# A hybrid encoder layer on one core: heads' products in pairs, weights loaded by events, a third fill tile, packed constants, five prepared down steps

## The chip, the cores and the metric

One core of one Trainium2 chip. The metric is the device time of one execution in microseconds. TensorE (PE) multiplies, VectorE (DVE) and ScalarE (ACT) work on tiles in SBUF and PSUM, GpSimd (POOL) does small steps, and SyncE (SP) issues nearly all transfers, in its own order.

## What is computed

One encoder layer over 16 tiles of 128 positions (two sequences of 1024, model width 1024). The core of the reference:

```python
h = rms_norm(x, norm1)
q, k, v, gu, gv = split(h @ w_in)                 # widths 512, 128, 128, 512, 512
a = rms_norm(windowed_gqa(q, k, v, q_gain, k_gain, sink, rel_table), attn_out_gain)
g = rms_norm(chunked_spatial_gating(gu, gv, v_gain, w_s, b_s), gmlp_out_gain)
x = x + concatenate([a, g]) @ w_o
h2 = rms_norm(x, norm2)
x = x + (silu(h2 @ w_gate) * (h2 @ w_up)) @ w_down   # inner width 2816
...
# windowed_gqa: 8 heads of 64, 2 key/value heads, block of 128 queries against 3 blocks of keys
scores = q . k / sqrt(64) + bias[rel], masked to |rel| <= 128
e = exp(scores - m);  probs = e / (sum(e) + exp(sink - m));  out = probs @ v
```

## The kernel before

Every product is made of three: operands are split into a high and a low part by `split` or `split_gain` (L111 on ScalarE gives the high part, L112 on VectorE the low one), and `mm3` (L221 to L223) multiplies high by high, low by high and high by low. In the projections these are fp32 forms, in the products of probabilities with v (L484 to L486) and in the FFN f16 forms.

**Start.** For k = 0 to 7 the k-th slice of x of the first four tiles and of the q weights (`load_wq`) is loaded, split and multiplied. Seven small constants come in by seven transfers: g1s on SP, the others on POOL's queue. Then the bias of relative positions is built: a row of it is written to DRAM, read back shifted, and turned by eight products (`bias_turn`, L291, L292).

**Attention.** A list of events, each with a time, is sorted and then run; the order of the calls is the order on every engine. `AT` holds the offsets, and tile t's work is put at 8 t plus an offset. Per tile: load and split x (`load_x`, L180, `split_x_hi`, L185), project it in 13 pieces (`fill`), norm and turn q and k (`qk_turn`: products pk, pt, L374 and L377), and for each of four head pairs hp the scores (L418), maximum (L423), exponential (L439), the split of the probabilities in f16 (`turn`, L463 and L464), their transpose by a transfer on SP (`turn_dma`, L471), and `pv`, the products of the transposed tile pT with v into po, nine for each head. The two heads of a pair are two events, 1.0 apart, so that other work can stand between them. `finish` and `finish2` norm the result and store it.

**gMLP weights.** At the event for tile 13 `load_gw("gv", ...)` issues four loads (L518) and eight splits one behind the other; `load_gw("gu", ...)` follows when all events have run (the scheduler still mixes its instructions with those of the last tiles, slots permitting). The staging tiles are of kind XL, of which there are three, shared with x. `NFILL = 2` tiles' products pgv (of the gMLP's v part) are put as fill between the last tiles' products; the other tiles' pgv, and all pgu, come behind the last tile, each with 24 products.

**Down product.** Its operands are the activations, split by a factor (asr) that needs the sum of squares of a whole sequence: `all_sum` (L1276), then a power on POOL. For the first `LEAD = 4` steps the half of sequence 0 is prepared early (`down_prep`, staging load L1309, splits L115 and L116) and multiplied (`down_mm`, L1347 to L1349, four banks); the half of sequence 1 is kept in a list `late` until the second factor is there.

Lines that set the order of work around the change:

```python
at(T + 8 + h + AT["pv"], lambda t, h: att[t].pv(h % 2 * GROUP + h // 2), t, h)
...
st = k4("XL", f"as{i}_{p}", (P, 2, 512))
load(st, act_d[i][:, blocks[p]])
...
for n in range(LEAD):
    down_mm(banks, [ready[n]], n == 0, False, False, (0,))
    if n == 1:
        act_scale(1)
for fn in late:
    fn()
...
for n in range(LEAD):
    down_mm(banks, [ready[n]], n == 0, False, False, (1,))
```

Of the kernel before, what the change touches and what calls it, by code (L numbers as in the profile page):

```python
# [16 lines left out]
P = 128  # L17
# [15 lines left out]
NFILL = 2  # L33
# [11 lines left out]
    loadx=-35.779, xhi=-32.464, xlo=-28.937, rsum=-32.424, rpow=-28.393, proj=-23.482, pstep=0.544, evac=0.096, qksum=-16.778,  # L45
    scale=-12.309, turnq=-12.228, hi=-10.123, lo=-7.358, sc=0.193, tr=3.514, trd=5.452, pv=1.792, ex=3.273,
    norm=7.726, norm2=16.428, finish=17.892, finish_pow=18.192, finish2=38.679, gmf=-23.874, gmstep=1.931, ld_gv=-2.058, st1=-3.154,
    st2=11.546,
)


@with_exitstack
def kernel(
# [10 lines left out]
    bsT: bass.AP,  # L64
    g1: bass.AP,
    go: bass.AP,
    n2: bass.AP,
    qg2: bass.AP,
    kg2: bass.AP,
    sink: bass.AP,  # L70
# [57 lines left out]
    ones = k4("S", "ones", (P, P))  # L128
    nc.gpsimd.memset(ones, 1.0)

    def const(name, shape, src, eng=nc.gpsimd):
        t = cp.tile(list(shape), F32, name=name)
        eng.dma_start(t, src)
        return t

    g1s = const("g1s", [P, KD], g1, nc.sync)
    qgs = const("qgs", [P, 1], qg2)
    kgs = const("kgs", [P, 1], kg2)
    sks = const("sks", [P, NH], sink.to_broadcast([P, NH]))
    gos = const("gos", [P, KD], go)  # L140
    n2s = const("n2s", [P, KD], n2)
    bss = const("bss", [P, NH], bsT)
# [145 lines left out]
    def bias_turn():  # L288
        for h in range(NH):
            ps = xx(f"pj{h}", [P, 384])  # L290
            nc.tensor.matmul(ps, rev, shifted[h // 2][:, h % 2], start=True, stop=True)  # L291
            nc.vector.tensor_copy(bias[:, h], ps)  # L292
# [6 lines left out]
    nc.tensor.matmul(ps_v, ones, vss, start=True, stop=True)  # L299
# [98 lines left out]
    class Attn:  # L398
# [113 lines left out]
    def load_gw(nm_, c0):  # L512
        hi = h16(f"w{nm_}_hi")
        lo = h16(f"w{nm_}_lo")
        wgl[nm_] = (hi, lo)
        for k0 in range(0, KD, 2):
            st = k4("XL", f"st{nm_}{k0}", (P, 2, 512))
            load(st, w_in_v[:, k0 : k0 + 2, c0 : c0 + 512])  # L518
            for j in range(2):
                k = k0 + j  # L520
                split_gain(hi[:, k, :], lo[:, k, :], st[:, j, :], g1s[:, k : k + 1])
# [53 lines left out]
    at(-0.95, bias_turn)  # L575
    for t in range(NT):
        T = 8.0 * t
        if t < GROUP:
            at(-20.0 + t, lambda t: run(proj_pieces(t)), t)
            at(-16.0 + t + AT["st1"], proj_evac, t)  # L580
            at(-16.0 + t + AT["st1"], qk_sum, t)
# [7 lines left out]
        if t == NT - 3:  # L589
            at(T + AT["ld_gv"], load_gw, "gv", 1280)  # L590
        if t >= GROUP:
            at(T + AT["loadx"], load_x, t)
            at(T + AT["xhi"], split_x_hi, t)
            at(T + AT["xlo"], xlo, t)
            at(T + AT["rsum"], rstd1_sum, t)
            at(T + AT["rpow"], rstd1_pow, t)
            for k in range(13):
                at(T + AT["proj"] + k * AT["pstep"], fill, t, 1)
            at(T + AT["proj"] + 12 * AT["pstep"] + AT["evac"], proj_evac, t)
            at(T + AT["qksum"], qk_sum, t)  # L600
        if t >= GROUP - 1:
            at(T + AT["scale"], qk_scale, t)
            at(T + AT["turnq"], qk_turn, t)
            at(T + AT["hi"], qk_hi, t)
            at(T + AT["lo"], qk_lo, t)
        at(T - 0.01, start_attn, t)
        for h in range(NH):
            at(T + 8 + h + AT["pv"], lambda t, h: att[t].pv(h % 2 * GROUP + h // 2), t, h)
            if h % 2:
                at(T + h - 0.5 + AT["sc"], lambda t, h: att[t].scores(h // 2), t, h)  # L610
                at(T + h + AT["ex"], lambda t, h: att[t].exps(h // 2), t, h)
                at(T + h + AT["tr"], lambda t, h: att[t].turn(h // 2), t, h)
# [16 lines left out]
    load_gw("gu", 768)  # L629
# [33 lines left out]
    def gm_group(gi):  # L663
        us, vh, vl = grp[gi]
        for h in range(NH):
# [6 lines left out]
            for c2 in range(2):  # L672
# [3 lines left out]
                )  # L676
        for c in range(GROUP):
# [19 lines left out]
    def wo_gain():  # L697
        one = k4("S", "ones2", (P, P))
        nc.gpsimd.memset(one, 1.0)
        ps = xx("ps_w", [P, KD])  # L700
        nc.tensor.matmul(ps, one, wss, start=True, stop=True)
# [150 lines left out]
    nc.scalar.activation(n2j, n2s, AF.Square, accum_out=n2ss)  # L852
# [3 lines left out]
    nc.vector.tensor_scalar_mul(n2s, n2s, n2r[:, 0:1])  # L856
# [450 lines left out]
    def down_prep(i, p, late=None):  # L1307
        st = k4("XL", f"as{i}_{p}", (P, 2, 512))
# [42 lines left out]
    LEAD = 4  # L1351
# [103 lines left out]
def _layout(inputs):  # L1455
# [54 lines left out]
```

## Time and profile before

| what | value |
|---|---|
| median of 3 runs | 1870.58 us (1869.58 to 1872.12) |
| the profiled execution | 1869.99 us, of which span 1868.1 |
| mean granted TensorE clock | 0.991 |
| busy: PE, DVE, ACT, POOL | 1827.9, 1160.2, 1007.8, 109.2 us |
| products | 9696 |

The span is the time from the first instruction to the last; the rest of an execution's time lies around it. Busy time is a sum over all stages; what a stage is bound by is read from windows. A gap is idle time of an engine just before an instruction, put down to what ended it. A clock of 1.00 is 2.4 GHz, 0.50 is 1.2 GHz, and a value between is a mixture of both within the stretch.

### The profile page before, as it was taken

How to read it: one execution, taken by the hardware profiler on the slowest of the kernel's cores; microseconds unless marked ns; L12 is line 12 of the kernel's file. 1: busy time of each engine (PE TensorE's matmuls, PEld its weight loads, DVE VectorE, ACT ScalarE, POOL GpSimd, SP SyncE). 2: the span in 40 equal slices, each digit the busy share in tenths (PEclk: the TensorE clock that was granted, in tenths of full speed). 3: DMA queues.
4: the chain of work that ended last, by engine and by line, in shares of the span. 5: the costliest groups of instructions: out<-in, count | busy, mean ns of one | idle time of the engine just before them, and what ended most of it. 6: DMA issues, size and time to landing. Idle time of an engine off the chain costs nothing.

```text
span 1868.1 us, 26075 instructions
## 1 busy us (share of the span) xinstructions
PE 1827.9 (98%) x9696; PEld 994.0 (53%) x9696; DVE 1160.2 (62%) x2183; ACT 1007.8 (54%) x1917; POOL 109.2 (6%) x149
## 2 busy tenths in 40 slices
PE   8999989999999989999999999999999999999999
PEld 7677767878555444444444444444444444444444
DVE  4887875573877887555645645645556856555661
ACT  6798978663666775534534534534444453333340
POOL 3122100110100000000000000000000000000000
PEclk9999989999999999999999999999999999999999
DMA  7798878442467875323313313313262654333641
GB/s 241 150 194 174 182 162 264 165 150 75 167 223 249 283 245 199 119 76 123 118 55 127 123 41 118 113 63 113 85 240 99 236 198 137 112 101 102 234 138 46
DMA packets 216207, 282.05 MB, mean 151 GB/s; under 512 B 103282, under 2 KB 138098, under 8 KB 216080
## 3 DMA queue, kind: packets, MB, share of 16 engines
q1 hardware_dynamic: 215632, 280.02, 47.9%
q8 instruction: 76, 1.25, 0.3%
q10 hardware_dynamic: 144, 0.26, 0.1%
q14 instruction: 51, 0.42, 0.1%
q0 software_dynamic: 304, 0.10, 0.0%
HBM read 177.04 MB, written 80.23 MB: 138 GB/s over the span
## 4 chain that ended last, share of the span: by engine, by line
PE 58%; DVE 2%; DMA 2%; issue 2%; ACT 1%; POOL 0%; POOLq 0%; SPq 0%; DVEq 0%; ACTq 0%
PE pd L1349 7%; PE pd L1347 7%; PE pd L1348 7%; PE pa L1073 4%; PE pa L1075 4%; PE pa L1074 4%; PE pd L1073 4%; PE pd L1074 4%; PE pd L1075 4%; PE pc L1073 4%; PE pc L1074 4%; PE pc L1075 4%; PE pb L1073 2%; PE pb L1074 2%; PE pb L1075 2%
## 5 line engine op out<-in xcount | busy, mean ns | idle before, releaser
L1347 PE MATMUL pd<-wop,a 128*128 128x512 f16 x616 | 234.1, 380 | 2.1 <-ACT a L115 2.1
L1349 PE MATMUL pd<-wop,a 128*128 128x512 f16 x616 | 234.1, 380 | 0.1
L1348 PE MATMUL pd<-wop,a 128*128 128x512 f16 x616 | 234.1, 380 | 0.0
L1074 PEld LDWEIGHTS <-op 128*128 128x128 f16 x1232 | 120.5, 98 | 148.8 <-issue 7.2
L1075 PEld LDWEIGHTS <-op 128*128 128x128 f16 x1232 | 120.5, 98 | 146.3 <-issue 1.2
L1073 PEld LDWEIGHTS <-op 128*128 128x128 f16 x1232 | 122.3, 99 | 142.9
L1073 PE MATMUL pa<-top,op 128*128 128x512 f16 x352 | 133.4, 379 | 0.7 <-ACT ua L1191 0.6
L1074 PE MATMUL pa<-top,op 128*128 128x512 f16 x352 | 133.4, 379 | 0.0
L1075 PE MATMUL pa<-top,op 128*128 128x512 f16 x352 | 133.4, 379 | 0.0
L115 ACT ACTIVATE wop<-wd,wdr_r 128x512 f16<-128x512 f32 x66 | 47.3, 720 | 154.2 <-PE pd L1349 151.2
L115 ACT ACTIVATE a<-as,asr_r 128x512 f16<-128x512 f32 x154 | 101.9, 708 | 33.9 <-DMA as<-act_d 17.8
L116 DVE SCALAR_TENSOR_TENSOR a<-as,asr_r,a 128x512 f16<-128x512 f32 x154 | 108.8, 746 | 8.8 <-ACT a L115 8.8
L1202 ACT COPY ub<-pc 128x512 f32<-128x512 f32 x44 | 25.7, 584 | 160.3 <-PE pc L1075 160.3
L116 DVE SCALAR_TENSOR_TENSOR wop<-wd,wdr_r,wop 128x512 f16<-128x512 f32 x66 | 49.2, 749 | 100.6 <-ACT wop L115 100.6
L1347 PEld LDWEIGHTS <-a 128*128 128x128 f16 x616 | 60.5, 98 | 75.3 <-ACT a L115 2.6
L1349 PEld LDWEIGHTS <-a 128*128 128x128 f16 x616 | 60.3, 98 | 73.7 <-DVE a L116 1.0
L1348 PEld LDWEIGHTS <-a 128*128 128x128 f16 x616 | 60.4, 98 | 72.7 <-issue 0.5
L1016 ACT ACTIVATE junk_e<-g 128x1024 f32<-128x1024 f32 x44 | 46.4, 1053 | 74.2 <-DVE g L1186 74.2
L439 ACT ACTIVATE sc<-sc,mx 128x384 f32<-128x384 f32 (+1 forms) x128 | 74.5, 584 | 12.5 <-DVE mx L423 12.3
L1208 DVE TENSOR_TENSOR ub<-ub,ua 128x512 f32<-128x512 f32 x44 | 30.4, 691 | 81.7 <-ACT ub L1202 79.2
L1183 ACT ACTIVATE g<-g,rs 128x512 f32<-128x512 f32 x57 | 41.1, 721 | 62.5 <-DVE g L1218 35.5
L423 DVE CUSTOM_DVE_ANT_0 sc<-ps,bias 128x384 f32<-128x384 f32 (+1 forms) x128 | 62.4, 520 | 16.0 <-PE ps L418 13.9
(377 smaller groups left out, 4600.7 us busy)
## 6 DMA issues: line engine op xcount, KB each, us to landing
as<-act_d SPq DMA_DIRECT2D x77, 512.0 KB, 3.4
act_d<-g SPq DMA_DIRECT2D x66, 256.0 KB, 2.0
xs<-in_xT_dram SPq DMA_DIRECT2D x28, 512.0 KB, 4.3
tr<-t_d SPq DMA_DIRECT2D x28, 512.0 KB, 5.2
raw<-in_wg_dram SPq DMA_DIRECT2D x24, 512.0 KB, 3.7
raw<-in_wu_dram SPq DMA_DIRECT2D x24, 512.0 KB, 4.6
act_d<-sa SPq DMA_DIRECT2D x44, 256.0 KB, 2.4
act_d<-sb SPq DMA_DIRECT2D x44, 256.0 KB, 2.7
```

The costliest lines, as they stand in the source:

```text
L115: nc.scalar.mul(hi, src, gain)
L116: nc.vector.scalar_tensor_tensor(lo, src, gain, hi, ALU.mult, ALU.subtract)
L423: nc.vector.tensor_tensor_reduce(out=sc[:, v, :W], in0=ps[v][:, :W], in1=bias[:, h, self.off : self.off + W], scale=1.0, scalar=-NEG, op0= ...
L439: nc.scalar.activation(sc[:, v, :W], sc[:, v, :W], AF.Exp, bias=self.mn[:, h : h + 1], scale=-1.0, accum_out=self.sums[:, h : h + 1],)
L1016: nc.scalar.activation(junk_e[0], src, AF.Square, accum_out=acc)
L1073: nc.tensor.matmul(ps, op[:, 0, k, :], th[:, k, :], start=first and k == 0, stop=False, **more)
L1074: nc.tensor.matmul(ps, op[:, 0, k, :], tl[:, k, :], start=False, stop=False, **more)
L1075: nc.tensor.matmul(ps, op[:, 1, k, :], th[:, k, :], start=False, stop=last and k == 3, **more)
L1183: nc.scalar.activation(dst, src, AF.Silu, scale=iv)
L1347: nc.tensor.matmul(ps, a[:, 0, s, cs], wop[:, 0], start=first and n == 0, stop=False, **kw)
L1348: nc.tensor.matmul(ps, a[:, 0, s, cs], wop[:, 1], start=False, stop=False, **kw)
L1349: nc.tensor.matmul(ps, a[:, 1, s, cs], wop[:, 0], start=False, stop=end, **kw)
```

## The change

Both heads of a pair are one `pv` event. The gMLP weights' loads and splits become separate events with times of their own, for gu as well as for gv. `NFILL` is 3. The offsets in `AT` are other numbers, and a table `TW` adds a shift for single tiles to the classes A (attention), Q (norm and turn of q and k) and R (load and projection). The bias products are eight events, in the order of heads 0, 4, 1, 5, 2, 6, 3, 7. The seven small constants are laid side by side on the host as one input of 128x42 and come in by one transfer on SP; the two inputs of the bias table are loaded on SP behind the first q weights; three tiles of ones become one, made at the start. `gm_group` is cut by `yield`, but run at once as before. In the down product `LEAD` is 5, and the early steps 1 and 3 stage in XN slots.

```diff
-NFILL = 2
+NFILL = 3
+PT_L = (0, 3)
+PG = 1
...
-    norm=7.726, norm2=16.428, finish=17.892, finish_pow=18.192, finish2=38.679, gmf=-23.874, gmstep=1.931, ld_gv=-2.058, st1=-3.154,
-    st2=11.546,
+    norm=6.71, norm2=11.259, finish=17.507, finish_pow=17.97, finish2=40.676, gmf=-26.818, gmstep=2.858, ld_gv=-5.686, st1=1.728,
+    ld_gu=21.124, sp_gv=-2.88, sp_gu=25.516, gvstep=0.02, gustep=0.288, bias=-3.338, biasstep=0.673, st2=11.369,
 )
+
+TW = {
+    ("A", 0): 0.425, ("A", 1): -0.02, ("A", 2): -0.026, ("A", 3): -0.012, ("A", 4): 0.017, ("A", 5): 0.003,
...
-    ones = k4("S", "ones", (P, P))
-    nc.gpsimd.memset(ones, 1.0)
...
-    g1s = const("g1s", [P, KD], g1, nc.sync)
-    qgs = const("qgs", [P, 1], qg2)
...
+    cst = cp.tile([P, 3 * KD + 2 * NH + 2], F32, name="cst")
+    nc.sync.dma_start(cst, consts)
...
+        if k == 0:
+            nc.gpsimd.memset(tabs, NEG)
+            load(tabs[0:32, :], tab)
+            load(oh, onehot)
...
-    def load_gw(nm_, c0):
...
+    def load_gw(nm_, j):
+        c0 = {"gv": 1280, "gu": 768}[nm_]
+        gst[nm_, j] = k4("XL", f"st{nm_}{j}", (P, 2, 512))
+        load(gst[nm_, j], w_in_v[:, 2 * j : 2 * j + 2, c0 : c0 + 512])
+
+    def split_gw(nm_, k):
+        if k == 0:
+            wgl[nm_] = (h16(f"w{nm_}_hi"), h16(f"w{nm_}_lo"))
+        hi, lo = wgl[nm_]
+        split_gain(hi[:, k, :], lo[:, k, :], gst[nm_, k // 2][:, k % 2, :], g1s[:, k : k + 1])
...
-    at(-0.95, bias_turn)
+    for n in range(NH):
+        at(AT["bias"] + n * AT["biasstep"], bias_turn, n % 2 * GROUP + n // 2)
     for t in range(NT):
         T = 8.0 * t
+        R, Q, A = (T + TW.get((c, t), 0.0) for c in "RQA")
...
         if t == NT - 3:
-            at(T + AT["ld_gv"], load_gw, "gv", 1280)
+            for nm_ in ("gv", "gu"):
+                for k in range(KD):
+                    if k % 2 == 0:
+                        at(T + AT["ld_" + nm_] + k * AT[nm_ + "step"], load_gw, nm_, k // 2)
+                    at(T + AT["sp_" + nm_] + k * AT[nm_ + "step"], split_gw, nm_, k)
...
-            at(T + 8 + h + AT["pv"], lambda t, h: att[t].pv(h % 2 * GROUP + h // 2), t, h)
             if h % 2:
+                at(A + 7.5 + h + AT["pv"], lambda t, h: [att[t].pv(v * GROUP + h // 2) for v in range(NKV)], t, h)
...
-        st = k4("XL", f"as{i}_{p}", (P, 2, 512))
+        st = k4("XN" if late is not None and p % 2 else "XL", f"as{i}_{p}", (P, 2, 512))
...
-    LEAD = 4
+    LEAD = 5
```

What the tables move is seen in the order of instructions. First TensorE in the middle of attention, where tile 5's products with v stand beside tile 9's projection (pq9) and the turn of tile 8's q and k (pk8, pt8); a row is a line of the kernel, an instruction, output<-inputs. Before:

```order
L486 LDWEIGHTS pT5_0_1908
L486 MATMUL po5_2015<-v0_416,pT5_0_1908 128x64
L221 MATMUL pq9_1983<-wq_hi_176,xh9_1697 128x512
L222 MATMUL pq9_1983<-wq_lo_177,xh9_1697 128x512
L223 MATMUL pq9_1983<-wq_hi_176,xl9_1811 128x512
L374 MATMUL pk8_2075<-ident_75,qk8_1871 128x128
L377 MATMUL pt8_2077<-ident_75,qk8_1871 128x128 x4
L221 MATMUL pq9_1983<-wq_hi_176,xh9_1697 128x512
L222 MATMUL pq9_1983<-wq_lo_177,xh9_1697 128x512
L223 MATMUL pq9_1983<-wq_hi_176,xl9_1811 128x512
L484 LDWEIGHTS pT5_1_1978
```

and now:

```order
L486 LDWEIGHTS pT5_0_1876
L486 MATMUL po5_2043<-v0_405,pT5_0_1876 128x64
L374 MATMUL pk8_2065<-ident_75,qk8_1865 128x128
L377 MATMUL pt8_2067<-ident_75,qk8_1865 128x128 x4
L221 MATMUL pq9_1958<-wq_hi_165,xh9_1682 128x512
L222 MATMUL pq9_1958<-wq_lo_166,xh9_1682 128x512
L223 MATMUL pq9_1958<-wq_hi_165,xl9_1753 128x512
L221 MATMUL pq9_1958<-wq_hi_165,xh9_1682 128x512
L222 MATMUL pq9_1958<-wq_lo_166,xh9_1682 128x512
L223 MATMUL pq9_1958<-wq_hi_165,xl9_1753 128x512
L221 MATMUL pq9_1958<-wq_hi_165,xh9_1682 128x512
```

Before, nine products with v (the last of them in the first two rows) stand between pieces of the projection; now 18 stand in a row, and the projection's pieces behind them.

Second SP's queue at the end of attention (pT12_1: transposed probabilities of tile 12, pair 1; stgv, stgu: gMLP weights; xs: x of a fill tile). Before:

```order
L508 DMA mix_a10_115<-o10_3503 128x512
L518 DMA stgv6_3648<-in_w_in_dram 128x2x512
L180 DMA xs1_3706<-in_xT_dram 128x1024
L518 DMA stgu0_4393<-in_w_in_dram 128x2x512
L471 DMA_TRANSPOSE pT12_1_3735<-ph12_1_3670 128x12x128
L518 DMA stgu2_4399<-in_w_in_dram 128x2x512
L471 DMA_TRANSPOSE pT12_2_3785<-ph12_2_3737 128x12x128
```

and now:

```order
L508 DMA mix_a10_104<-o10_3481 128x512
L517 DMA stgv3_3502<-in_w_in_dram 128x2x512
L180 DMA xs1_3672<-in_xT_dram 128x1024
L180 DMA xs2_3866<-in_xT_dram 128x1024
L471 DMA_TRANSPOSE pT12_1_3698<-ph12_1_3658 128x12x128
L517 DMA stgu0_4237<-in_w_in_dram 128x2x512
L471 DMA_TRANSPOSE pT12_2_3754<-ph12_2_3722 128x12x128
```

Two loads of x now stand ahead of pT12_1, and the first load of gu's weights behind it.

Third TensorE at the down stage's entry (a0_n and wop0_n: the operands of step n; banks pd0_0 to pd0_3 are of sequence 0, pd0_4 to pd0_7 of sequence 1; psasr1: the product for the second factor). Before:

```order
L1276 MATMUL psasr1_13948<-asum1_6116,onec_5996 128x22
L1347 LDWEIGHTS a0_2_13843
...
L1349 LDWEIGHTS a0_2_13843
L1349 MATMUL pd0_3_13923<-wop0_2_13844,a0_2_13843 128x512
L1347 LDWEIGHTS a0_0_13794
L1347 MATMUL pd0_4_13991<-wop0_0_13795,a0_0_13794 128x512
```

and now:

```order
L1282 MATMUL psasr1_13946<-asum1_6102,onec_85 128x22
L1353 LDWEIGHTS a0_2_13829
...
L1355 LDWEIGHTS a0_4_13880
L1355 MATMUL pd0_3_13921<-wop0_4_13881,a0_4_13880 128x512
L1353 LDWEIGHTS a0_0_13780
L1353 MATMUL pd0_4_14003<-wop0_0_13781,a0_0_13780 128x512
```

Before, sequence 1's first product follows three steps' products of sequence 0 (the fourth step's come later, since its staging tile has no slot yet); now it follows five steps'.

## Rows read from the trace of the kernel before

**Rows 1.** The page: busy us of each engine over the span (share) and count; and the clock granted to TensorE in 40 equal slices, in tenths.

```profile
PE 1827.9 (98%) x9696; PEld 994.0 (53%) x9696; DVE 1160.2 (62%) x2183; ACT 1007.8 (54%) x1917; POOL 109.2 (6%) x149
PEclk9999989999999999999999999999999999999999
```

**Rows 2.** The list of TensorE's waits over the span: engine, what waits <- what it waits for: us in total, times, longest.

```profile
PE po L484 <- DMA pT<-ph: 7.1, 5, 3.2
PE pd L1347 <- ACT a L115: 2.1, 1, 2.1
```

**Rows 3.** Windows of core 0: the stretch, its length in us, busy us of PE, PEld, DVE, ACT and POOL (each with its instructions), PEclk, DMA share, GB/s.

```profile
100.00:150.00 50.00, 50.00 (x501) 38.51 (x497) 41.23 (x112) 46.63 (x109) 9.07 (x9) 1.00 0.91 197
240.00:250.00 10.00, 6.34 (x67) 4.18 (x63) 8.42 (x25) 8.83 (x22) 2.51 (x2) 0.80 1.04 229
250.00:260.00 10.00, 10.00 (x38) 6.50 (x39) 4.71 (x12) 2.19 (x6) 0.00 (x0) 0.50 0.70 157
300.00:310.00 10.00, 10.00 (x46) 8.29 (x45) 5.85 (x11) 10.00 (x21) 1.38 (x3) 1.00 0.86 309
```

**Rows 4.** TensorE's timeline at 100.7 us, where projection follows products with v; columns: start, us, engine, line, operation, output<-inputs, count, and in brackets the idle time before it with its releaser.

```profile
100.68 0.36 PE L221 MATMUL pkv<-wkv,xh 128*128 128x256 f32 x1
100.88 0.28 PE L222 MATMUL pkv<-wkv,xh 128*128 128x256 f32 x1
101.00 0.28 PE L223 MATMUL pkv<-wkv,xl 128*128 128x256 f32 x1
```

**Rows 5.** TensorE's instructions by line and shape: busy us, mean ns | idle before.

```profile
L221 PE MATMUL pq<-wq_hi,xh 128*128 128x512 f32 x96 | 45.5, 473 | 0.0
L222 PE MATMUL pq<-wq_lo,xh 128*128 128x512 f32 x96 | 38.7, 403 | 0.0
```

**Rows 6.** TensorE's timeline (columns as in rows 4): the five gaps between 240 and 300 us, and the first product of pgv2 and the first behind its last.

```profile
244.10 0.45 PE L418 MATMUL ps<-kh,qt 64*128 64x384 f32 x1 [0.47 <-DVE mx L423]
247.73 0.23 PE L484 MATMUL po<-v,pT 128*128 128x64 f16 x1 [3.19 <-DMA pT<-ph]
...
271.64 0.20 PE L484 MATMUL po<-v,pT 128*128 128x64 f16 x1 [0.89 <-DMA pT<-ph]
...
283.23 0.20 PE L484 MATMUL po<-v,pT 128*128 128x64 f16 x1 [1.71 <-DMA pT<-ph]
...
297.20 0.20 PE L484 MATMUL po<-v,pT 128*128 128x64 f16 x1 [1.16 <-DMA pT<-ph]
...
301.99 0.39 PE L221 MATMUL pgv<-wgv_hi,xh 128*128 128x512 f32 x1
...
307.43 0.39 PE L221 MATMUL pgu<-wgu_hi,xh 128*128 128x512 f32 x1
```

**Rows 7.** Windows (columns as in rows 3): two stretches at the end of attention, one in the FFN, one in the down stage.

```profile
248.00:263.00 15.00, 15.00 (x82) 10.29 (x79) 6.75 (x19) 6.54 (x16) 0.55 (x1) 0.50 0.61 142
283.00:291.00 8.00, 7.63 (x71) 6.15 (x72) 6.96 (x18) 5.83 (x15) 0.93 (x1) 0.57 0.85 187
589.00:593.00 4.00, 1.27 (x8) 0.72 (x7) 1.89 (x2) 1.11 (x2) 0.00 (x0) 1.00 1.03 385
1471.00:1475.00 4.00, 4.00 (x11) 1.46 (x12) 2.04 (x3) 1.16 (x2) 0.00 (x0) 0.57 0.56 187
```

**Rows 8.** SP's timeline (columns as in rows 4) ahead of the late transpose, the last row.

```profile
238.05 0.33 SPq L180 DMA_DIRECT2D xs<-in_xT_dram  x1
239.38 0.38 SPq L518 DMA_DIRECT2D stgu<-in_w_in_dram  x1
240.31 2.24 SPq L471 DMA_TRANSPOSE pT<-ph  x1
```

**Rows 9.** ScalarE's timeline at its long wait, and TensorE's in the slow stretch: the second product with v behind the late tile, and the first of three scores with the product behind the third (columns as in rows 4).

```profile
260.65 0.37 ACT L383 ACTIVATE kh<-pk,kgs 128x128 fp32r<-128x128 f32 x1 [8.46 <-PE pk L374]
...
247.78 0.24 PE L485 MATMUL po<-v,pT 128*128 128x64 f16 x1
...
250.44 0.69 PE L418 MATMUL ps<-kh,qt 64*128 64x384 f32 x1
...
251.70 0.80 PE L222 MATMUL pgv<-wgv_lo,xh 128*128 128x512 f32 x1
```

**Rows 10.** ScalarE: one split of x from the timeline (columns as in rows 4), and the group of copies from a gMLP product by line and shape (columns as in rows 5).

```profile
243.40 1.05 ACT L185 CAST xh<-xs 128x1024 fp32r<-128x1024 f32 x1 [1.17 <-DMA xs<-in_xT_dram]
...
L537 ACT ACTIVATE xg<-pgu,rstd_all 128x512 f32<-128x512 f32 x1 | 0.7, 669 | 0.0
```

**Rows 11.** TensorE's timeline at the down stage's entry (columns as in rows 4): the first product, the last before the wait, the first behind it.

```profile
1460.84 0.38 PE L1347 MATMUL pd<-wop,a 128*128 128x512 f16 x1
...
1468.53 0.38 PE L1349 MATMUL pd<-wop,a 128*128 128x512 f16 x1
1470.99 0.39 PE L1347 MATMUL pd<-wop,a 128*128 128x512 f16 x1 [2.08 <-ACT a L115]
```

**Rows 12.** The same place on ScalarE (the end of the last square) and VectorE (one split), columns as in rows 4.

```profile
1465.59 0.19 ACT L1016 ACTIVATION_READ_ACCUMULATOR junk_e<-g 128x1 f32 x1
...
1464.46 0.74 DVE L116 SCALAR_TENSOR_TENSOR wop<-wd,wdr_r,wop 128x512 f16<-128x512 f32 x1
```

**Rows 13.** The start: the first product (columns as in rows 4), and a window at the end of the start (columns as in rows 3).

```profile
6.15 0.79 PE L221 MATMUL pq<-wq_hi,xh_s 128*128 128x512 f32 x1 [6.15 <-ACT wq_hi L111]
...
60.00:65.00 5.00, 5.00 (x16) 2.87 (x15) 5.00 (x17) 4.37 (x16) 0.60 (x1) 0.50 1.11 225
```

More of the change, by code (lines that the diff above doesn't have):

```diff
@@ L127 @@
     nc.gpsimd.memset(pm[:, 1:2], 0.5)
-    ones = k4("S", "ones", (P, P))
-    nc.gpsimd.memset(ones, 1.0)
[L131 to L134, printed above, removed]
-    g1s = const("g1s", [P, KD], g1, nc.sync)
-    qgs = const("qgs", [P, 1], qg2)
[L138 to L142, printed above, removed]
+    onec = cp.tile([P, P], F32, name="onec")
+    nc.gpsimd.memset(onec, 1.0)
+    cst = cp.tile([P, 3 * KD + 2 * NH + 2], F32, name="cst")
+    nc.sync.dma_start(cst, consts)
+    g1s, gos, n2g = (cst[:, n * KD : (n + 1) * KD] for n in range(3))
+    sks, bss = (cst[:, 3 * KD + n * NH : 3 * KD + (n + 1) * NH] for n in range(2))
+    qgs, kgs = (cst[:, 3 * KD + 2 * NH + n : 3 * KD + 2 * NH + n + 1] for n in range(2))
+    n2s = cp.tile([P, KD], F32, name="n2s")
     qg8 = cp.tile([P, 1], F32, name="qg8")
@@ L286, with bias_turn @@
     bias = h16("bias", (P, NH, 384), F32)
[L288 to L292, printed above, removed]
+    def bias_turn(h):
+        ps = xx(f"pj{h}", [P, 384])
+        nc.tensor.matmul(ps, rev, shifted[h // 2][:, h % 2], start=True, stop=True)
+        nc.vector.tensor_copy(bias[:, h], ps)
     junk = k4("S", "junk", (P, KD, P))
@@ L298 @@
     ps_v = xx("ps_v", [P, 2])
-    nc.tensor.matmul(ps_v, ones, vss, start=True, stop=True)
+    nc.tensor.matmul(ps_v, onec, vss, start=True, stop=True)
     vtot = cp.tile([P, 1], F32, name="vtot")
@@ L510 @@
     wgl = {}
-    def load_gw(nm_, c0):
[L513 to L521, printed above, removed]
+    gst = {}
+    def load_gw(nm_, j):
[7 more added lines that the diff above has]
+        split_gain(hi[:, k, :], lo[:, k, :], gst[nm_, k // 2][:, k % 2, :], g1s[:, k : k + 1])
     pxg = {}
@@ new lines @@
+        if t >= GROUP:
+            at(R + AT["loadx"], load_x, t)
+            at(R + AT["xhi"], split_x_hi, t)
+            at(R + AT["xlo"], xlo, t)
+            at(R + AT["rsum"], rstd1_sum, t)
+            at(R + AT["rpow"], rstd1_pow, t)
+            for k in range(0, 13, PG):
+                at(R + AT["proj"] + k * AT["pstep"], fill, t, PG)
+            at(R + AT["proj"] + 12 * AT["pstep"] + AT["evac"], proj_evac, t)
+            at(Q + AT["qksum"], qk_sum, t)
+        if t >= GROUP - 1:
+            at(Q + AT["scale"], qk_scale, t)
+            at(Q + AT["turnq"], qk_turn, t)
+            at(Q + AT["hi"], qk_hi, t)
+            at(Q + AT["lo"], qk_lo, t)
@@ L663, in gm_group, with gm_group_pieces @@
     def gm_group(gi):
+        run(gm_group_pieces(gi))
+    def gm_group_pieces(gi):
         us, vh, vl = grp[gi]
@@ L697, in wo_gain @@
     def wo_gain():
-        one = k4("S", "ones2", (P, P))
-        nc.gpsimd.memset(one, 1.0)
         ps = xx("ps_w", [P, KD])
-        nc.tensor.matmul(ps, one, wss, start=True, stop=True)
+        nc.tensor.matmul(ps, onec, wss, start=True, stop=True)
         tot = small("m", 1)
@@ L851 @@
     n2j = small("sums", KD)
-    nc.scalar.activation(n2j, n2s, AF.Square, accum_out=n2ss)
+    nc.scalar.activation(n2j, n2g, AF.Square, accum_out=n2ss)
     ps_n2 = xx("ps_n2", [P, 1])
@@ L1466, in per_part @@
         return v.reshape(-1, P).T
+    both = [np.concatenate([a[k]] * 2, axis=1).reshape(P, 1) for k in ("q_gain", "k_gain")]
+    sink = np.broadcast_to(a["sink"].reshape(1, NH), (P, NH))
+    gains = np.concatenate([a["attn_out_gain"], a["gmlp_out_gain"]], axis=1)
+    consts = [per_part(a["norm1"]), per_part(gains), per_part(a["norm2"]), sink, a["b_s"][0].T, *both]
+    consts = np.concatenate(consts, axis=1)
     arrays = [
```

57 lines of the change are left out of this document (14 added, 43 removed), and 6 rows, old and new, of the table TW.

## The prediction

> **What bounds the kernel now.** The page's first two parts come first: TensorE is busy 98% of the span, VectorE 62%, ScalarE 54%, and the granted clock falls below its upper level in only a few slices [rows 1]. So the kernel ends when TensorE has worked off its queue, and a change is worth what it takes from TensorE's queue, from its waits, or from the time at the lower clock. The list of TensorE's waits is short: the product with v behind a transposed tile, 7.1 us in five waits, and the down product behind a split activation, 2.1 us [rows 2]. The windows by 10 us then show where clock and waits meet. From 100 to 150 us TensorE is busy 50.00 of 50.00. At the end of attention, 240 to 300 us, it is busy 6.34 of 10 in one slice and runs at 0.50, that is at 1.2 GHz instead of 2.4, in the next [rows 3]. Nearly all that can be won beside pure queue length lies there, at the down stage's entry, and in the first 65 us.
>
> **Heads in pairs.** The products with v are small: 64 columns, their starts 0.03 us apart. The fp32 product behind such a block starts at once, but the next one follows only after 0.20 us, where the same product is followed after 0.12 us otherwise [rows 4]. So leaving a block costs 0.08 us. For the wider q product the mean of the first of three is 473 ns against 403 for the second, 70 ns more over all 96 [rows 5]. By starts it is 0.087 us there, and I add 0.01 for the way in. In TensorE's order a block of products with v is left 105 times before and 66 times after. 39 x 0.09 = 3.5 us, all on the path, since TensorE has no idle time there [rows 3]. Bounds: nothing, if the load of the new operand is hidden after all; and, if all of the 70 ns x 96 = 6.7 us is due to the 58 blocks left for q, 0.116 each, 39 x 0.116 = 4.5 us. I take 3.5, since starts measure it directly.
>
> The Trainium skill says otherwise (TensorE: Matmul & The Clock Gate, "Step-by-step: what each phase is for"): TensorE pulls the load of the next stationary operand ahead, so that it runs under the current product. By that rule leaving a block would cost nothing and this term would be 0; the row that shows 0.20 for 0.12 us speaks against it.
>
> **The end of attention.** What it costs now: five gaps of 0.47, 3.19, 0.89, 1.71 and 1.16 us, 7.4 in all [rows 6], and two stretches at the lower clock: 15 us at 0.50, 7.5 us lost, and 8 us at 0.57, 3.4 us lost [rows 7]. Together 18.3 us; that is the most there is to be won.
>
> The first gap is a transposed tile (pT12_1) that is late on SP's in-order queue: loads of 512 KB each (gMLP weights, x, gMLP weights; the last two at 238.05 and 239.38) are issued ahead, and the transpose only at 240.31, its issue itself taking 2.24 us [rows 8]. After the change three such loads still stand ahead of it (one of weights, two of x). So I leave this gap, 3.7 with the 0.47 ahead of it.
>
> What changes lies behind it. ScalarE stands still for 8.46 us until 260.65, because its next instruction needs pk15, which TensorE reaches only then, at half speed [rows 9]. In the new order 13 products with v and 5 scores fewer stand between the late tile and pk15: by starts 13 x 0.053 + 5 x 0.42 = 2.8 us at the lower clock [rows 6, 9]; at the upper one pk15 is reached at about 252, and the whole 8.46 us go. The third fill tile costs ScalarE a split of x of 1.05 us and a copy of 0.67 [rows 10], so its chain to the last transposed tile comes 1.1 to 6.7 us earlier; I take 5. At the same time 24 products of pgv2, which now follow the last product with v (301.99 to 307.43, 5.4 us of work without a wait [rows 6]), stand between the blocks of tiles 14 and 15. Together they remove the gaps of 0.89, 1.71 and 1.16 us, 3.8 in all, and the second slow stretch, which began right behind the 1.71 gap: 3.4. Of the first slow stretch I count half, 3.75: the rows don't say that a wait lowers the clock. Between 589 and 593 us TensorE was idle for 2.7 us with the clock at 1.00 [rows 7]. Against this stands a new wait: the last 6 products of pgu0 need the split of the last gMLP weights, which now stands on ScalarE behind the evacuation of tiles 13 and 14; 0 to 2 us, I take 1. Sum 3.8 + 3.4 + 3.75 - 1 = 10 us, bounds 3 (only the smaller gaps) and 18.3.
>
> **The down stage.** Three steps' first halves (36 products) run from 1460.84 to 1468.75; then TensorE waits 2.08 us for the second half's first split at 1470.99 [rows 11], which waits for POOL's factor: the sum's product needs ScalarE's last square, at 1465.8, and behind it come a reduction, two small steps and POOL's power [rows 12]. Behind the wait 4 us run at 0.57: 1.7 us lost [rows 7]. After, five steps' first halves (60 products, 0.216 each) last 13.0 us from the same start, to 1473.8, and the first split is there at 1470.99. Two more splits (0.7 each on VectorE [rows 12]) come ahead of that chain, and two subtractions of 0.6 go behind it; even if all of 1.4 us hits it, 1472.4 is early enough. The two new staging tiles load early, and the residual loads that used those slots go later, with over 100 us until they are needed. So both go: 2.1 + 1.7 = 3.8, bounds 2 (the wait alone) and 4.2.
>
> **The start.** One constants load on SP takes the place of one on SP and six on POOL's queue. The first product waits 6.15 us for the first split weights [rows 13]; one load of constants stands ahead of those weights on SP in both orders, now a wider one, whose issue can take some tenths more. The bias products, 8 in a row before, are put between the transposes; VectorE still makes the same 8 copies before the first scores. From 60 to 65 us the clock stands at 0.50 [rows 13]; if the more even order lifted it, 2.5 us would go. I take 0.3, bounds -1 and 2.5. Where the gMLP weights' events, the generator and the new names move nothing on TensorE, they cost nothing: SP and VectorE are idle around them, and if their cover went, the price would be the one of the late tile.
>
> Sum: 3.5 + 10 + 3.8 + 0.3 = 17.6 us off the profiled execution's 1869.99, so 1852.4; the median of the runs stands 0.6 above that execution, so **1853.0**.
>
> **Rivals.**
> (a) The late tile is as late, the lower clock stays through its whole stretch, and ScalarE gains only 1.1 us. For it: the same three loads ahead. Against it: the 24 products that fill the gaps. Tail 3 instead of 10: 1860.0.
> (b) The pairs save nothing, because the load of the next operand is hidden under the product before. That is the sum without its first term: 1856.5. The row of 0.20 against 0.12 [rows 4] speaks against it. This is the way the rule quoted above from the Trainium skill (TensorE: Matmul & The Clock Gate) would have it.
> (c) The clock stays up, in the tail and from 60 to 65 us, and the gaps go: 18.3 + 2.5 + 3.5 + 3.8 = 28.1, so 1842.5. For it: an idle time of 2.7 us left the clock at 1.00 [rows 7]. Against it: the largest gap is not removed.
> (d) Slower, by SP's queue. Transposes share it with loads that wait for a slot; the second x load is new ahead of pT12_1, and a weights load ahead of pT13_2. A load that waits holds every transpose behind it, and TensorE, in order, waits as long. The price of one such stop is by the rows 3.19 + 7.5 = 10.7 us. One more leaves the change faster by 7; from the second on (21.4, more than 17.6) it is slower, and three give 1885; with two 1874. For it: the DMA share of 1.04 in that slice [rows 3]. Against it: six of the weights' splits, which give slots back, stand ahead of tile 12's second turn on ScalarE in both orders.
> (e) The tail's gain is given back: from 300 to 310 us ScalarE is busy 10.00 of 10.00 [rows 3]; if the gMLP stage is ScalarE's and not TensorE's, TensorE arrives early and waits. Between 1860 and 1870.
>
> **How the numbers follow.** The forecast 0.42, (a) 0.18, (b) 0.10, (c) 0.12, (e) 0.10, (d) 0.08. A measurement tells about 0.2%, 3.7 us, from no change. Faster by more: the forecast, (a), (b), (c) and 0.04 of (e), 0.86; within it the rest of (e), 0.06; slower (d), 0.08. The range: the forecast, (a), (b) and (c) make 0.82, so from 1842 to 1862, 2 us past (a), whose price is the least sure.
>
> **What would show it.** Right: in the down stage no wait for the activation's split and a clock of 1.00 from 1450 on; a second x load on SP ahead of pT12_1; ScalarE's wait for pk15 below 5.5 us; the second clock drop gone; in the lists by shape the q product's first of three nearer the other two. Wrong: a wait for pT13 or pT14 over 3 us, a new wait of pgu on ScalarE's split over 2 us, or a clock at 0.50 for more than 17 us between 240 and 300. If the down stage keeps its wait, the psasr1 step is late, and 3.8 of the sum is gone.

## The result, and the profile after

The changed kernel takes 1855.8 us (median of 4 runs, 1853.4 to 1858.8) against 1870.9 beside it, so the medians lie 15.1 us apart. The ratio on record is 0.9914, 95% interval 0.9900 to 0.9927, which makes it 16.1 us. A second set of runs gave 0.9911 (0.9895 to 0.9927). The forecast was 17.6 us. The profiled execution took 1855.08 us, its span 1853.3, which is 14.8 us shorter than before.

How far the changed kernel is ahead, by the same instruction in both traces (the first product's start or the last product's end):

| point | before | after | gained so far |
|---|---|---|---|
| first product | 6.15 | 5.64 | 0.5 |
| last product with v of tile 11 | 240.73 | 233.65 | 7.1 |
| first product of pgu2 (attention is over) | 307.43 | 290.29 | 17.1 |
| first product of the gate of tiles 4 to 7 (sg1) | 387.14 | 369.62 | 17.5 |
| last product of pgu15 | 468.15 | 455.50 | 12.7 |
| first down product | 1460.84 | 1450.38 | 10.5 |
| end of the span | 1868.1 | 1853.3 | 14.8 |

So 17.5 us are won by the gate, 7.0 of them are lost again before the down stage, and 4.3 more are won there. The page, answering to [rows 1]:

```profile
PE 1815.3 (98%) x9696; PEld 992.3 (54%) x9696; DVE 1158.5 (63%) x2183; ACT 1009.5 (54%) x1918; POOL 106.1 (6%) x139
PEclk9999999999999999999999999999999999999999
```

TensorE's waits, answering to [rows 2] (columns as there): the product with v waits 4.9 us instead of 7.1, the down product's wait is gone, and the gate (sg) now waits 4.5 us in one piece.

```profile
PE sg L679 <- DVE u L684: 5.4, 3, 4.5
PE po L484 <- DMA pT<-ph: 4.9, 3, 2.9
```

Windows, answering to [rows 3, 7, 13] (columns as there):

```profile
58.00:66.00 8.00, 8.00 (x53) 5.35 (x53) 8.00 (x27) 7.97 (x26) 1.07 (x1) 1.00 0.87 194
100.00:150.00 50.00, 50.00 (x514) 39.30 (x514) 43.39 (x123) 47.33 (x114) 10.65 (x10) 1.00 0.99 208
248.00:252.00 4.00, 4.00 (x26) 2.61 (x24) 2.88 (x9) 3.84 (x12) 0.00 (x0) 0.57 0.74 143
282.00:286.00 4.00, 3.04 (x18) 2.56 (x19) 2.19 (x5) 1.46 (x5) 0.21 (x1) 0.57 1.00 384
374.70:381.60 6.90, 5.91 (x20) 5.26 (x21) 5.40 (x19) 3.02 (x6) 0.00 (x0) 0.51 0.25 76
644.00:648.00 4.00, 4.00 (x20) 3.08 (x19) 2.36 (x2) 4.00 (x13) 0.00 (x0) 0.57 0.73 228
1440.00:1480.00 40.00, 40.00 (x188) 18.26 (x187) 37.43 (x63) 20.15 (x32) 1.07 (x1) 1.00 0.79 262
```

The slow stretch at 58 us is gone, the one at 248 (17 us long before, 15 of it in the window) is now 3.4 long (4 us at 0.57), the one at 283 half as long as before, and two new ones stand at 375 and 644 us. In the down stage the clock is 1.00 and TensorE is never idle. TensorE's timeline at the gaps, answering to [rows 6, 11] (columns as in rows 4), with the gate's wait and the first products of pgu2 and of the down stage:

```profile
242.06 0.44 PE L418 MATMUL ps<-kh,qt 64*128 64x384 f32 x1 [0.81 <-DVE mx L423]
...
246.84 0.20 PE L484 MATMUL po<-v,pT 128*128 128x64 f16 x1 [1.16 <-DMA pT<-ph]
...
267.66 0.20 PE L484 MATMUL po<-v,pT 128*128 128x64 f16 x1 [0.79 <-DMA pT<-ph]
...
282.95 0.23 PE L484 MATMUL po<-v,pT 128*128 128x64 f16 x1 [2.95 <-DMA pT<-ph]
...
290.29 0.39 PE L221 MATMUL pgu<-wgu_hi,xh 128*128 128x512 f32 x1
...
375.69 0.55 PE L679 MATMUL sg<-vh,ws_hi 128*128 128x256 f32 x1 [4.48 <-DVE u L684]
...
1450.38 0.38 PE L1353 MATMUL pd<-wop,a 128*128 128x512 f16 x1
```

At the end of attention the gaps sum to 5.7 us against 7.4 [rows 6]: the large one for tile 12 is gone (its last pair waits 1.16), and a large one for tile 15 has come. The lower clock costs 1.7 + 1.7 there against 10.9 [rows 7]. So of the 10 us won in that place, most is clock.

### The profile page after: what moved, and what is told of

Same layout as the page of the kernel before. It is cut to its first block, busy times and chain, and to the rows that moved or that the text cites. A ratio compares the mean times of both kernels' runs of the same rounds, so it can differ in the third digit from the quotient of the medians.

```text
span 1853.3 us, 26039 instructions
## 1 busy us (share of the span) xinstructions
PE 1815.3 (98%) x9696; PEld 992.3 (54%) x9696; DVE 1158.5 (63%) x2183; ACT 1009.5 (54%) x1918; POOL 106.1 (6%) x139
## 4 chain that ended last, share of the span: by engine, by line
PE 61%; DVE 2%; DMA 1%; ACT 1%; issue 0%; SPq 0%; POOL 0%; DVEq 0%
PE pd L1353 7%; PE pd L1355 7%; PE pd L1354 7%; PE pd L1079 4%; PE pd L1080 4%; PE pd L1081 4%; PE pa L1079 4%; PE pc L1079 4%; PE pa L1080 4%; PE pc L1080 4%; PE pc L1081 4%; PE pa L1081 4%; PE pb L1079 2%; PE pb L1080 2%; PE pb L1081 2%; DMA tr<-t_d 1%
## 5 line engine op out<-in xcount | busy, mean ns | idle before, releaser
L1079 PE MATMUL pd<-top_6h,op 128*128 128x512 f16 x176 | 66.7, 379 | 3.9 <-ACT ub L1212 3.7
```

Of the source, the lines that this page charges most:

```text
L1079: nc.tensor.matmul(ps, op[:, 0, k, :], th[:, k, :], start=first and k == 0, stop=False, **more)
```

## Experiments

Ratios are to the kernel before in the same runs; the changed kernel's is 0.9911 to 0.9914. Each interval is about 0.0015 to either side, 2.8 us, so the difference of two such ratios is uncertain by some 4 us (an estimate: two independent errors of 2.8), and where a difference is that small the place in the trace decides.

**Heads apart, and heads in pairs alone.** The pair's event split into two in the changed kernel; and, in the kernel before, two events made one.

```diff
+            at(A + 8 + h + AT["pv"], lambda t, h: att[t].pv(h % 2 * GROUP + h // 2), t, h)
             if h % 2:
-                at(A + 7.5 + h + AT["pv"], lambda t, h: [att[t].pv(v * GROUP + h // 2) for v in range(NKV)], t, h)
```

> The changed kernel, with the two heads of a pair as two events again, 1.0 apart around the pair's time; all else as changed. TensorE's order then leaves a block of products with v 110 times instead of 66 (44 more). Theory (a switch costs 0.09 us by starts): 4 us slower than the changed kernel, about 1860. Rival (the load of the next operand is hidden): no difference, 1856. Second rival: a late transposed tile or the clock at the end of attention moves, then the windows from 240 to 290 us differ and not those from 100 to 200.

> The kernel before with both heads of a pair in one event, nothing else changed. TensorE's order leaves a block of products with v 63 times instead of 105 (42 fewer). Theory (0.09 us each): 3.8 us faster than before, about 1867, seen from 66 to 240 us. Rival (hidden load): no difference. The second half of a block now waits for the later of two transposed tiles, so waits at the end of attention may grow by up to 3 us.

Apart: 1859.4 us, 0.9935 (0.9921 to 0.9950), about 4 us more than the changed kernel; in the trace the last product of pgu3 ends 5.3 us later, 0.7 of it from the start. Alone: 0.9988 (0.9977 to 0.9999), 2.2 us less than before. The clearest measure is the stretch from the last product with the k and v weights (pkv) of tile 4 to that of tile 14, in which TensorE does the same work at a clock of 1.00, and without a wait in all but the second row:

| kernel | from | to | length, us | blocks left |
|---|---|---|---|---|
| before | 73.90 | 222.11 | 148.21 | 70 |
| before, heads in pairs | 74.03 | 221.08 | 147.05 (0.53 of it waits) | 40 |
| changed | 70.51 | 214.77 | 144.26 | 40 |
| changed, heads apart | 71.32 | 220.87 | 149.55 | 71 |

The same order repeats its length within 0.04 us from profile to profile. So in the new order the pairs are worth 5.3 us over these ten tiles, 0.17 per block, and in the old one 1.2 (1.7 without the new waits), 0.06 per block; 0.09 was forecast. Heads apart in the new order take 1.3 us longer than before, with one block more, so the number of blocks alone does not set the length. The traces show a like price at other changes: a q product is followed by a score after 0.326 us and by another q product after 0.232, and with the pairs alone ten blocks stand ahead of scores, which start 0.123 us after the block's last product instead of 0.029. (Both heads of a pair read the same transposed tile, so there is no later one of two to wait for.) The q product's first of three, by line and shape (columns as in rows 5), with the heads apart:

```profile
L221 PE MATMUL pq<-wq_hi,xh 128*128 128x512 f32 x96 | 44.7, 466 | 0.0
L222 PE MATMUL pq<-wq_lo,xh 128*128 128x512 f32 x96 | 37.8, 394 | 0.0
```

and in the changed kernel:

```profile
L221 PE MATMUL pq<-wq_hi,xh 128*128 128x512 f32 x96 | 42.1, 439 | 0.0
L222 PE MATMUL pq<-wq_lo,xh 128*128 128x512 f32 x96 | 37.7, 393 | 0.0
```

The first of three falls from 466 to 439 ns, the second stays. So leaving a block costs time, and the rival, no difference, is out; the second rival is out too, since the loss grows from tile to tile, from 0.8 us at tile 4 to 6.1 at tile 14. What in TensorE takes the time no run here separates.

**Four down steps, and five alone.** `LEAD = 4` and XL staging put back; and `LEAD = 5` with XN staging put into the kernel before.

```diff
-        st = k4("XN" if late is not None and p % 2 else "XL", f"as{i}_{p}", (P, 2, 512))
+        st = k4("XL", f"as{i}_{p}", (P, 2, 512))
...
-    LEAD = 5
+    LEAD = 4
```

> The changed kernel with four prepared down steps and all staging in XL slots again. Theory: the wait for the activation's split (2.1 us) and the slow stretch behind it (1.7 us) come back, 3.8 us slower than the changed kernel, about 1859.6. Rival: the late second factor was cured by something ahead of the down stage, then no more than 1 us and no wait. Second rival: the slow stretch does not hang on the wait, then 2.1.

> The kernel before with five prepared down steps, steps 1 and 3 staged in XN slots. Theory: wait and slow stretch at the down stage go, 3.8 to 4.2 us faster than before, about 1867. Rival: the part needs the other parts' times, then under 1 us. Its attention is the one of before, so its profile is a third look at the slow stretches there.

Undone: 1859.7, 0.9936 (0.9922 to 0.9951), about 4.2 us more. Alone: 0.9983 (0.9973 to 0.9994), 3.2 less. With four steps the wait is there again (list of waits),

```profile
PE pd L1353 <- ACT a L121: 2.1, 1, 2.1
```

and the slow stretch behind it (window):

```profile
1464.50:1468.00 3.50, 3.50 (x10) 1.19 (x9) 0.95 (x2) 0.07 (x2) 0.00 (x0) 0.52 0.78 254
```

and with five in the kernel before, TensorE is busy throughout at the upper clock:

```profile
1440.00:1480.00 40.00, 40.00 (x190) 18.41 (x189) 32.95 (x61) 19.77 (x33) 2.44 (x3) 1.00 0.54 181
```

The part stands by itself and gives what was forecast: from the first down product to the end it takes 402.9 us in the changed kernel, 403.1 with five steps in the kernel before, 407.2 before and with four steps put back. The slow stretch is not sure to follow the wait: two other profiles with four steps (the kernel before a second time, and with pairs alone) have the same wait of 2.08 us, no slow stretch behind it, and take 406.1. So the part is worth 3.1 to 4.3 us.

**Two fill tiles.** `NFILL = 2` in the changed kernel.

> The changed kernel with two fill tiles instead of three; the times of all events as changed. Theory (pgv2 fills the gaps of the last tiles): the waits for pT14 and pT15 grow by 3 to 5.4 us, and a slow stretch of 3.4 comes back: 5 to 9 us slower than the changed kernel, 1861 to 1865. Rival (the new times and the weights' events alone brought the tail's gain, and ScalarE's chain is shorter without the third tile): within 2 us, 1854 to 1858.

1857.5, 0.9929 (0.9915 to 0.9943), 2.8 us more, which is within the noise; in the trace attention's work ends 1.0 us later (1.3 at pgu3, 0.3 of it from the start). The theory is out: the third tile is worth about 1 us, not the tail.

**The kernel before, a second time.**

> The kernel before, profiled a second time. Theory (the slow stretches at the end of attention belong to the order of work there): again about 17 us at half speed from 246 us and 7 us from 283, and 7 us from 58. Rival (a wait makes a slow stretch likely, and whether and how long is chance): the gaps recur within 0.5 us each, but the stretches have other lengths or are missing, and the time moves by half of the difference in their length.

1872.2 us. The windows of the second profile (columns as in rows 3), and behind them those of the kernel before with five down steps, whose attention is the same:

```profile
245.00:262.00 17.00, 15.82 (x84) 11.01 (x84) 8.49 (x22) 8.77 (x23) 1.03 (x2) 0.50 0.65 156
282.00:289.00 7.00, 6.31 (x72) 5.23 (x73) 6.25 (x18) 5.09 (x14) 0.48 (x1) 0.76 0.75 168
50.00:58.00 8.00, 7.05 (x30) 4.81 (x30) 7.00 (x18) 2.48 (x6) 1.70 (x1) 0.79 0.01 2
58.00:66.00 8.00, 6.72 (x49) 4.65 (x48) 8.00 (x26) 7.37 (x25) 1.53 (x2) 1.00 0.71 148
```

```profile
245.00:262.00 17.00, 15.41 (x83) 10.71 (x84) 7.32 (x20) 7.78 (x18) 0.56 (x2) 0.50 0.60 142
```

The stretch at 245 us is 17 us long in all three profiles of the old order and in none of the ten of the new one: it belongs to the order. The others change their length or place: in the second profile the one at 58 us is 3.4 us at 50, the one at 283 is 3.4 instead of 6.8. With the pairs alone the long one is 10.2 us.

**Bias products in one event.** In the changed kernel.

```diff
-    for n in range(NH):
-        at(AT["bias"] + n * AT["biasstep"], bias_turn, n % 2 * GROUP + n // 2)
+    at(-0.95, lambda: [bias_turn(h) for h in range(NH)])
```

> The changed kernel with the eight bias products in one event at -0.95, as before; all else as changed. Theory (the spread bias products keep TensorE from waiting at 58 us and so from the slow stretch of 6.8 us there): 3 to 4 us slower than the changed kernel, with gaps of 0.5 to 0.7 at 56 to 59 us and a clock of 0.50 behind. Rival (the new times of the first tiles did it, or chance): within 1 us.

1857.5, 0.9928 (0.9914 to 0.9943), 2.6 us more, by time alone within the noise. In its trace 10.2 us run at half speed from 58.8:

```profile
58.80:69.00 10.20, 10.20 (x31) 6.58 (x30) 6.93 (x24) 7.20 (x22) 1.07 (x1) 0.50 0.73 180
```

With the products in a row, five of five profiles (of both orders) have a slow stretch of 3.4 to 10.2 us between 50 and 69; with them spread, four of nine have one, 3.4 long, at 48 to 52, and the others none.

**The output weights behind the gate.** The scaling of their steps 2 and 3 takes a copy of the gain that hangs on the gate's result (`u1` is the last eight columns of tile 7's gate, times 0.0):

```diff
-            nc.scalar.mul(r, r, wgain[:, j : j + 1])
+            nc.scalar.mul(r, r, (wgain, wgain2)[k > 1][:, j : j + 1])
...
             gm_group(t // GROUP - 1)
+            if t == 9:
+                u1 = grp[1][0][1][:, 1, GW - KD : GW]
+                nc.vector.scalar_tensor_tensor(wgain2, u1, 0.0, wgain, ALU.mult, ALU.add)
```

> The changed kernel, with the scaling of the output weights of steps 2 and 3 made to depend on the gate of tiles 4 to 7, by a small VectorE step that copies their gain; so VectorE's order has the gate's 16 steps ahead of these weights' splits. Theory (TensorE's new wait of 4.48 us at 371 us, and the 6.8 us at half speed behind it, come from VectorE standing behind weights that are late): both go, 7.9 us faster than the changed kernel, about 1848. Rival (TensorE is only early, and waits elsewhere for the same weights or for x): the wait moves behind 376 us, and the time stays within 1.5 us of 1856. Between: the wait goes and the clock falls elsewhere, 4.5 us.

In the kernel before, the gate waited too, but less (TensorE's timeline):

```profile
391.00 0.35 PE L669 MATMUL sg<-vh,ws_hi 128*128 128x256 f32 x1 [2.28 <-ACT wo1h L107]
```

1851.6, 0.9890 (0.9874 to 0.9907), about 4.3 us less than the changed kernel, which is the middle case. In the changed kernel VectorE's timeline shows the split of late weights, and behind it the gate's step (u), for which TensorE had finished by 371.2:

```profile
374.34 0.69 DVE L114 TENSOR_TENSOR wo3l<-wr,wo3h 128x512 f16<-128x512 f32 x1
374.94 1.38 DVE L684 SCALAR_TENSOR_TENSOR u<-sg,cst,u 128x128 f32<-128x128 f32 x5
```

With the edit TensorE is not idle there, and the clock stays up:

```profile
370.00:382.00 12.00, 12.00 (x66) 10.38 (x65) 7.67 (x29) 6.21 (x15) 2.74 (x5) 1.00 0.28 107
```

At the end of the gMLP stage it is 7.0 us ahead of the changed kernel, near the 7.9 forecast; in its profile 3.5 of these are lost in the O stage and FFN, with slow stretches at 574 and 639 us (the changed kernel's has one there, at 644).

**The weights in blocks.** One event for gv's loads and splits, gu's behind all events (`load_all` is four loads and eight splits one behind the other).

```diff
...
-            for nm_ in ("gv", "gu"):
-                for k in range(KD):
-                    if k % 2 == 0:
-                        at(T + AT["ld_" + nm_] + k * AT[nm_ + "step"], load_gw, nm_, k // 2)
-                    at(T + AT["sp_" + nm_] + k * AT[nm_ + "step"], split_gw, nm_, k)
+            at(T + AT["sp_gv"], load_all, "gv")
...
+    load_all("gu")
     ws_hi = k4("L", "ws_hi", (P, NH, P), F32R)
```

> The changed kernel with the gMLP weights in blocks again: gv's loads and splits in one event at the time at which the splits stand now, gu's behind all events as before. All other times as changed. Theory (the end of attention gained by the new times of the attention's events, and the order of ScalarE and SP around tiles 12 and 13 is nearly the same with blocks): within 1.5 us of the changed kernel. Rival (the weights' own events keep ScalarE and SP free there): the long slow stretch at 246 us and a wait of 3 us for tile 12 come back, 5 to 10 us slower, 1861 to 1866.

1850.6, 0.9888 (0.9871 to 0.9905): 4.6 us less than the changed kernel, which neither expected. What differs is VectorE's order ahead of tile 15's last transpose. Its operand is made by ScalarE (high part) and VectorE (low part). In the changed kernel (columns as in rows 4; the last row is SP's issue of the transpose):

```profile
271.42 0.60 ACT L463 CAST ph<-sc 128x512 f16<-128x512 f32 x1
...
271.78 1.41 DVE L118 SCALAR_TENSOR_TENSOR wgu_lo<-stgu,cst,wgu_hi 128x512 fp32r<-128x512 f32 x2
...
273.17 1.41 DVE L118 SCALAR_TENSOR_TENSOR wgu_lo<-stgu,cst,wgu_hi 128x512 fp32r<-128x512 f32 x2
274.50 0.69 DVE L464 TENSOR_TENSOR ph<-sc,ph 128x512 f16<-128x512 f32 x1
...
275.26 1.26 SPq L471 DMA_TRANSPOSE pT<-ph  x1
```

and with blocks:

```profile
270.75 0.61 ACT L463 CAST ph<-sc 128x512 f16<-128x512 f32 x1
...
271.51 0.69 DVE L464 TENSOR_TENSOR ph<-sc,ph 128x512 f16<-128x512 f32 x1
...
272.26 1.24 SPq L471 DMA_TRANSPOSE pT<-ph  x1
```

In the changed kernel the high part is done at 272.02, but VectorE has four splits of gu's weights to do first and begins the low part at 274.50. SP issues the transpose 0.07 us after the low part ends; the store of tile 12's result and the loads ahead of it on SP had been issued by 274.68, so SP's queue held nothing back. With blocks the low part begins 0.15 us after the high part, and the transpose goes out 3.0 us earlier; TensorE's product follows it after 4.9 us instead of 7.7, and what shortened the transfer was not separated. TensorE's wait of 2.95 us is 0.43, no slow stretch follows, and attention's work ends 5.0 us earlier. Of these, 1.6 us are won by the end of tile 12, because this profile has no slow stretch at 248 us, and that can be chance: a second profile of the changed kernel, below, has none there either. The rest recurs. In seven profiles with the weights' events and three fill tiles or fewer the low part begins 2.3 to 3.1 us after its high part, in the one with four fill tiles 0.7, and in the six with blocks or in the old order 0.2 to 0.4.

**The changed kernel again.**

> The changed kernel again, profiled and timed beside the kernel before. Theory (where a wait leaves the clock low is partly chance): the gaps at 376, 283 and 247 us recur within 0.7 us, the slow stretches at 248, 283, 375 and 644 us recur only in part, and the time is 1853 to 1859. Rival: all four recur with the same length.

1855.0, 0.9911. The gaps are 0.88, 3.17 and 4.33 us at 247, 283 and 376 (in the first profile 1.16, 2.95 and 4.48); slow stretches at 283, 376 and 642, and one at 48, but none at 248: chance has its part.

**A fourth fill tile**, on top of the output weights behind the gate: `NFILL = 4`.

> The kernel with the output weights behind the gate, and a fourth fill tile. Theory (TensorE's last wait in attention, 2.9 to 3.6 us for tile 15's last transposed tile, is covered by the fourth tile's products): 3 to 5 us faster than without the fourth, 1847 to 1849. Rival (ScalarE's chain to that tile gets a split and a copy more, 1.7 us, and TensorE runs out of cover as before, since the third tile moved the end by 1 us only): within 1.5 us of 1851.6.

1849.6, 0.9885 (0.9866 to 0.9904), against 0.9890: the rival's time. TensorE's wait for tile 15 is 1.88 instead of 3.4 us, but one of 1.52 for tile 14 has come, and attention's work ends at the same time.

**Blocks and gate together.**

> The changed kernel with both earlier edits: the gMLP weights in blocks, and the output weights behind the gate. Theory (two separate waits, one for tile 15's last transposed tile and one for VectorE at the gate): the gains of 4.4 and 4.5 us add up, 1846 to 1848, ratio to the kernel before about 0.9865, and TensorE's list of waits has neither a wait of 3 us for pT nor one of 4 us for sg. Rival (the second wait only takes up time that the first gives): about 1850, 0.989.

1845.5 us (1843.1 to 1846.4), 0.9867 (0.9851 to 0.9884): 25 us faster than before, 8.5 faster than the change. The two gains add up, so the two waits are separate.

```profile
PE po L484 <- DMA pT<-ph: 3.0, 4, 0.9
...
PE sg L682 <- DVE u L687: 0.9, 2, 0.7
```

## Why the prediction was right, and where it was not

- **Heads in pairs**, 3.5 us: the size fits, its working, 39 blocks at 0.09 us, does not. Over ten tiles the changed kernel is 4.0 us shorter than before with 30 blocks fewer. But a block's price is 0.17 us in the new order and 0.06 in the old, so the step that failed is the fixed 0.09 for each block: by the starts above, what stands on either side of a block counts as well. The time alone could not have told, since 1855.8 lies nearer to rival (b)'s 1856.5 than to 1853.0. By the rule quoted from the Trainium skill (TensorE: Matmul & The Clock Gate, "Step-by-step: what each phase is for") this term would be 0, and the runs do not agree: 5.3 us for 31 blocks.
- **The end of attention**, 10 us: right in size (17.1 less 7.1 is 10.0), by luck, for three steps of it failed. First, "so I leave this gap", and the reading behind it that pT12_1 was late on SP's queue. Before, VectorE made the low part of this tile behind five splits of gv's weights, which then ended at 240.22, and SP issued the transpose at 240.31:

```profile
235.96 3.39 DVE L112 SCALAR_TENSOR_TENSOR wgv_lo<-stgv,g1s,wgv_hi 128x512 fp32r<-128x512 f32 x5
239.27 0.95 DVE L464 TENSOR_TENSOR ph<-sc,ph 128x768 f16<-128x768 f32 x1
```

So the loads ahead of it on SP did not hold it. In the changed kernel three loads still stand ahead of it, but it is issued at 232.00 (against the last product with v of tile 11 that is 1.2 us earlier than before) and is there within 5.9 us instead of 7.4, and TensorE does not wait for it. Of the 3.7 us left in the sum 2.0 remain (0.81, and 1.16 for the tile's last pair). Second, the gaps of tiles 13 to 15 were to go, 3.8 us: 0.79 and 2.95 us, 3.7 in all, take their place, the large one because VectorE stood behind the splits of gu's weights, which are events of the change itself. Third, half of the first slow stretch was counted, 3.75 us, and 5.8 went, while of the second, counted whole with 3.4, half stayed. So gaps gave 1.7 us and not 3.8; the clock gave 7.5 and not 7.15. ScalarE's wait for pk15 is gone, as forecast. The third tile, which was to fill the gaps, is worth about 1 us, and the weights' own events cost 4.6. With heads apart, with two fill tiles and with the weights in blocks the stretch of 17 us stays away all the same. So it is by elimination that the new times of the attention's events brought the tail (the pairs alone, in the old order, shorten the stretch to 10.2 us); which of them ends it was not separated, and why TensorE runs at the lower clock for 17 us there stays open.
- **The new wait of pgu on gu's split**, 1 us: it did not come.
- **The down stage**, 3.8 us: right, 4.3 in the trace, about 4.2 by undoing it, 3.2 alone.
- **The start**, 0.3 us: too small. At 74 us the changed kernel is 3.4 us ahead, 0.7 of it by 43 us. The packed constants gave nothing that stands out (the first product comes at 5.57, 5.64 and 6.00 us in three further profiles of the old start, at 5.64 here), but the spread bias products mostly remove the slow stretch, which was only the upper bound: 2.7 us in the trace, 2.6 by undoing it.
- **Not in the sum**: 7.0 us given back. The gate waits 4.5 us instead of 2.3 and then 5.9 us of work run at half speed, 4.9 us lost; the other 2.2 us go in the O stage and FFN, 1.7 of them by the slow stretch at 644. Rival (e) named the stage, but its engine was wrong: VectorE's order, not ScalarE's load. Up to tile 11 and in the down stage the change won about 4 us more than forecast, which made up for more than half of these losses; that is why the sum came within 1.5 us by the ratio and 2.8 by the traces, and it is luck.
- Rival (d), transposes held on SP, did not happen: in the changed kernel the longest that a transpose is issued behind its low part is 1.7 us (tile 8), and TensorE waits for none that was held so.

## What to carry to other kernels

Where TensorE is the bound, look for its waits and its clock together: here waits of 2.1 to 4.5 us cost 0.6 to 0.8 as much again where a slow stretch stood behind them, and removing one such wait (4.3 and 4.6 us by the ratios) gave as much as all the pairs. When one stage becomes faster, look at once at the next place where another engine's fixed order puts late work ahead of what TensorE needs. Twice in the changed kernel this was VectorE, with splits of weights ahead of a short step that TensorE's next operand hung on, at the gate and at the last transposed tile. A late transfer looks like a matter of the queue that issues it; compare its issue with the end of the step that makes its data before you say so.

## What the runs showed of the hardware that was not expected

The same wait is followed by a slow stretch in one execution and not in another. In the changed kernel the wait of 2.29 us that ends at 643.7 us is followed by 3.4 us at half speed (the window at 644 above). With the heads apart the same wait, 2.28 us, ends at 646.4, and the clock stays up:

```profile
644.00:648.00 4.00, 1.72 (x15) 1.59 (x15) 0.83 (x2) 4.00 (x6) 0.55 (x1) 1.00 0.90 308
646.00:650.00 4.00, 3.58 (x25) 2.63 (x26) 2.36 (x2) 4.00 (x11) 0.00 (x0) 1.00 0.76 228
```

Each such stretch costs 1.7 us, and the runs of one kernel lie 2 to 10 us apart (the kernel before from 1866.0 to 1875.6 in 23 runs), so the length of a single profile can't tell differences of this size. The gaps recur better (3.19, 2.40 and 3.27 us for tile 12 in three profiles of the old order, 2.95 and 3.17 for tile 15 in two of the changed kernel), and stretches without a wait recur best: the ten tiles above take 148.21, 148.25 and 148.21 us in three profiles of the old order, and 144.26 in four of the new. By contrast the stretch of 17 us in the old order came in three profiles of three.
